# HGRN2 decays inside the chunk: differences of cumulated sums on VectorE, or sums by TensorE with constant 0/1 matrices

## The chip, the cores and the metric

One core of one Trainium2 chip runs the whole program. The metric is device microseconds from start to end of an execution; the median of three runs is quoted. Weights and constants lie in DRAM when the clock starts.

## The reference, cut to what matters

Two layers of a diffusion backbone over 512 latent and 256 context tokens, width 1024. In each layer a combined projection feeds four mixers of four heads of 64 channels: HGRN2, RWKV-7, windowed attention and latent attention. HGRN2 is a gated linear attention in both directions, computed in chunks of 64 tokens:

```python
bc = jnp.cumsum(blocks(logf), axis=-2)            # log decays, cumulated within a chunk
def step(S, inp):
    qb, kb, vb, bb = inp
    inter = jnp.einsum('bhtk,bhkv->bhtv', qb * jnp.exp(bb), S)
    rel = jnp.where(causal, bb[:, :, :, None, :] - bb[:, :, None, :, :], -jnp.inf)
    att = jnp.einsum('bhtk,bhsk,bhtsk->bhts', qb, kb, jnp.exp(rel))
    o = inter + jnp.einsum('bhts,bhsv->bhtv', att, vb)
    b_end = bb[:, :, -1:, :]
    S = jnp.exp(b_end[:, :, 0, :, None]) * S + jnp.einsum('bhsk,bhsv->bhkv', kb * jnp.exp(b_end - bb), vb)
    return S, o
```

The second layer needs no output for context tokens, only their states.

## The kernel before, in words

The channels lie on the partitions and the tokens along the free axis. `mixers` (line 1279) runs a layer's mixer half. It projects (TensorE, weights split in two parts for three-pass products), and `hg_gates` (889) makes log decays and keys of both directions; line 926 cumulates the decays within chunks with a scan. Then, in pools opened at line 1437, `weave` (243) traces several streams side by side: RWKV forward and RWKV backward (`rw_dir`, one step each per round), HGRN (`hgrn`, 0.44 step per round in the first layer and 0.36 in the second), the preparation of the attentions, and in the first layer the rest of the modulation vectors (`ada`). The place of an instruction in an engine's queue comes from a scheduler that takes the traced order as priority; a queue is worked in order. The next stage (the attentions and the read-out, from line 1462 on) opens its PSUM pool when the streams have ended; its first products are those of line 338.

RWKV (`rw_pair` 685, `rw_chain` 795) inverts triangular matrices of two chunks by doubling: per level products of a<-TP,Gm, a copy into the padded AP (607), products a<-AP,TT, the update of TU (781), its turn on TensorE (312) and copies (785, 791).

HGRN (`hgrn` 928) goes through six segments of four chunks, three per direction, the context segment first. Per segment:

- keys scaled to the end of their chunk: a difference (962), an exponential (963), a product (964), turned on TensorE to `ket` (968 to 971); `ef`, the exponential of the cumulated decays (966);
- if output is wanted, six levels (976): for level h the causal pairs whose tokens lie in the later and the earlier half of a block of 2h tokens. A difference against a reference token of each block (983), two exponentials of the two halves (995, 996), the keys' product (997), the queries' product into the padded operand XQ, one instruction per partition half (1000), the products of scores in PSUM (1013), and a masked copy into `att` (1015). Level 0 takes pairs with the diagonal (987 to 990, 1003 to 1008);
- the states of the four chunks (1020 to 1029) and the output (1032 to 1044).

"Padded" means that an operand holds both head halves along a further free index and is zero where that index is not the partition half, so that the whole array contracts. HGRN's PSUM tag `hg` has two buffers of one bank; the attentions' preparation and `ada` draw on it as well. The program's float32 products show up as two records each in the trace, a turn as one.

Of the kernel before, what the change touches and what calls it, by code (L numbers as in the profile page):

```python
# [11 lines left out]
F32 = mybir.dt.float32  # L12
# [22 lines left out]
# columns of the per-layer parameter block  # L35
# [4 lines left out]
# columns of the constant block  # L40
# [4 lines left out]
NCST = C_BAND + 256  # L45


def _consts():
    """Constants that depend on shapes alone."""
# [40 lines left out]
    for n, cc, sc in ((64, C_COS, C_SIN), (32, C_COSM, C_SINM)):  # L90
# [3 lines left out]
        for p in range(128):  # L94
            d = p % n
            ang = pos[d // (n // 2)] * inv[d % nf]
            c[p, cc:cc + 512] = np.cos(ang)
            c[p, sc:sc + 512] = np.sin(ang)
    c[:, C_BAND:C_BAND + 128] = np.where(i[None, :] >= i[:, None], 0.0, -1e30)
# [4 lines left out]
def _col_tiles():  # L104
    """Column tiles (lists of w_in columns) that are computed channels x tokens, and the token-major group."""
# [17 lines left out]
# heads 0, 2, 1, 3  # L123
# [6 lines left out]
def _pack(inp):  # L130
# [7 lines left out]
    # shifts and scales of two channel tiles side by side  # L138
# [84 lines left out]
class Ker:  # L223
# [19 lines left out]
    def weave(*gens):  # L243
        """Traces several streams side by side: (generator, steps at a time)."""
# [31 lines left out]
    def gemm_col(s, ps, parts, act, segs):  # L276
        """ps[:, tokens] = weights^T act for one tile of 128 output channels.  parts: (first k, tiles) of the weights."""
# [7 lines left out]
    def gemm_last(s, m, *a):  # L285
        """Column m; the last one a segment after the other, as the norm of the first begins beside the second."""
# [3 lines left out]
    def gemm_cols(s, cols, act, ks=range(KT)):  # L290
        """The same for several column tiles (psum, parts, segments) together, k by k."""
# [8 lines left out]
    def diag(s, out, lhsT, rhs, start=True, stop=True):  # L300
        """64 x 64 products of the two partition halves, each with its own half."""
# [3 lines left out]
    def dtrans(s, out, x, idm):  # L305
        """64 x 64 transposes of the two partition halves."""
# [24 lines left out]
    def seg_gemm(s, lhsT, rhs, ntok, use, tag=None):  # L331
        """use(columns, psum) for each segment of lhsT^T rhs; lists of operands are summed."""
# [46 lines left out]
    def setup_masks(s):  # L379
        """The constants that the recurrences need."""  # L380
# [7 lines left out]
        # masks of the pairs that hold the diagonal as well  # L388
# [31 lines left out]
    def ada_rest(s, tp, room):  # L420
        """The first layer's second half and the second layer, a channel tile at a time, without the tensor engine.
        s.adaw(): where the weights of a tile go."""
# [4 lines left out]
        for n in range(72):  # L427
# [4 lines left out]
            # the second layer's context goes no further than its keys  # L432
# [12 lines left out]
    def sumsq(s, m, n, pool, x=None, eng=None):  # L445
        """Adds the squares of channel tile m of the residual to s.acc."""
# [31 lines left out]
    def norm(s, l, mod, sh, sc, gcol, wp, rs, hhi, hlo, ks, ts=None):  # L478
        """Channel tiles ks of the normalised and modulated residual in two parts; ts: room for two tiles."""
# [18 lines left out]
    def proj(s, l, cols, eng=None):  # L498
        """Column tiles (number, tokens) of the input projection into PSUM (channels x tokens); several at once go k by k."""
# [4 lines left out]
    def proj_tok(s, l, it, vt):  # L504
        """HGRN inputs and window values, tokens on partitions."""
# [39 lines left out]
    def rw_prep(s, l, last, g, tp):  # L545
        """Everything of the RWKV mixer that needs no state."""
# [34 lines left out]
        # values, centred over the channels of their head, tokens on partitions  # L581
# [9 lines left out]
        # bonus: (sum over the head of r k r_k) v  # L591
# [1379 lines left out]
```

## Time and profile before

| | us |
|---|---|
| runs, median (lowest to highest) | 2637.68 (2636.43 to 2646.11) |
| span of the profiled execution | 2644.5 |
| TensorE matmul busy | 2408.1 (91%) |
| VectorE busy | 1660.6 (63%) |
| ScalarE busy | 1227.3 (46%) |
| GpSimd busy | 484.9 (18%) |

The profiled execution is a run of its own; what lies around its span is not recorded beside it. Busy times are unions over the whole span and mix stages with different limits. L12 is line 12 of the kernel; PE and PEld are TensorE's matmuls and weight loads, DVE VectorE, ACT ScalarE, POOL GpSimd, SP the queue that issues most transfers. A group's row gives the count, the busy time, the mean length of one in ns, and after the second bar the engine's idle time just before, with what ended it.

### The profile page before, as it was taken

How to read it: one execution, taken by the hardware profiler on the slowest of the kernel's cores; microseconds unless marked ns; L12 is line 12 of the kernel's file. 1: busy time of each engine (PE TensorE's matmuls, PEld its weight loads, DVE VectorE, ACT ScalarE, POOL GpSimd, SP SyncE). 2: the span in 40 equal slices, each digit the busy share in tenths (PEclk: the TensorE clock that was granted, in tenths of full speed). 3: DMA queues.
4: the chain of work that ended last, by engine and by line, in shares of the span. 5: the costliest groups of instructions: out<-in, count | busy, mean ns of one | idle time of the engine just before them, and what ended most of it. 6: DMA issues, size and time to landing. Idle time of an engine off the chain costs nothing. (4 is left out here: it accounts for less than half of the span.)

```text
span 2644.5 us, 46379 instructions
## 1 busy us (share of the span) xinstructions
PE 2408.1 (91%) x18131; PEld 1998.6 (76%) x18131; DVE 1660.6 (63%) x3055; ACT 1227.3 (46%) x2331; POOL 484.9 (18%) x613
## 2 busy tenths in 40 slices
PE   6999788879998999999999997888996999999994
PEld 3889666656586888888888786666674898899993
DVE  5573598777578644344336746876745667667765
ACT  4373356546723211211234654664653556555653
POOL 1010464441011000000020005654102000000002
PEclk9999899989998999999999998998998899999997
DMA  6223110111053433334322130001113888888885
GB/s 245 65 89 111 49 34 20 30 65 57 1 178 129 144 112 120 117 116 132 118 81 64 57 116 13 20 16 49 56 36 107 267 270 270 280 265 264 260 277 179
DMA packets 161026, 322.46 MB, mean 122 GB/s; under 512 B 12288, under 2 KB 84736, under 8 KB 160800
## 3 DMA queue, kind: packets, MB, share of 16 engines
q1 hardware_dynamic: 153744, 293.60, 34.2%
q0 software_dynamic: 6480, 23.73, 2.5%
q8 instruction: 144, 2.36, 0.4%
q10 hardware_dynamic: 576, 2.10, 0.2%
q14 instruction: 82, 0.67, 0.1%
HBM read 295.39 MB, written 22.54 MB: 120 GB/s over the span
## 5 line engine op out<-in xcount | busy, mean ns | idle before, releaser
L272 PE MATMUL big<-hhi,hiw 128*128 128x512 f32 (+1 forms) x1504 | 520.8, 347 | 9.1 <-ACT hhi L491 4.6
L273 PE MATMUL big<-hlo,hiw 128*128 128x512 f32 (+1 forms) x1504 | 523.6, 348 | 2.4 <-DVE hlo L492 2.4
L274 PE MATMUL big<-hhi,low 128*128 128x512 f32 (+1 forms) x1504 | 519.5, 346 | 5.8 <-DVE low L260 3.9
L259 ACT CAST hiw<-raww 128x512 fp32r<-128x512 f32 (+3 forms) x208 | 158.4, 769 | 616.9 <-PE big L273 413.4
L272 PEld LDWEIGHTS big<-hhi,hiw 128*128 128x128 f32 x1504 | 286.2, 191 | 53.2 <-ACT hhi L491 5.7
L274 PEld LDWEIGHTS big<-hhi,low 128*128 128x128 f32 x1504 | 286.2, 190 | 45.1 <-DVE low L260 5.6
L273 PEld LDWEIGHTS big<-hlo,hiw 128*128 128x128 f32 x1504 | 286.4, 190 | 41.0 <-DVE hlo L492 4.2
L260 DVE TENSOR_TENSOR lom<-rawm,him 128x1024 fp32r<-128x1024 f32 x176 | 215.1, 1225 | 128.0 <-ACT him L259 126.7
L260 DVE TENSOR_TENSOR low<-raww,hiw 128x512 fp32r<-128x512 f32 (+3 forms) x196 | 177.3, 909 | 161.1 <-ACT hiw L259 160.8
L259 ACT CAST him<-rawm 128x1024 fp32r<-128x1024 f32 x176 | 184.3, 1047 | 150.4 <-PE sml L273 60.7
L272 PE MATMUL sml<-xh,him 128*128 128x256 f32 x528 | 152.0, 288 | 0.0
L273 PE MATMUL sml<-xl,him 128*128 128x256 f32 x528 | 149.5, 283 | 0.0
L274 PE MATMUL sml<-xh,lom 128*128 128x256 f32 x528 | 149.4, 283 | 0.0
L260 DVE TENSOR_TENSOR lov<-rawv,hiv 128x1024 fp32r<-128x1024 f32 x88 | 107.5, 1222 | 38.2 <-ACT hiv L259 37.8
L272 PE MATMUL sml<-him,xh 128*128 128x256 f32 x440 | 127.4, 290 | 0.7 <-DVE xl L260 0.6
L273 PE MATMUL sml<-lom,xh 128*128 128x256 f32 x440 | 125.4, 285 | 0.0
L274 PE MATMUL sml<-him,xl 128*128 128x256 f32 x440 | 125.3, 285 | 0.0
L273 PE MATMUL big<-gl,hiw 128*128 128x512 f32 (+1 forms) x352 | 119.5, 339 | 0.0
L272 PE MATMUL big<-gh,hiw 128*128 128x512 f32 (+1 forms) x352 | 118.9, 338 | 0.0
L274 PE MATMUL big<-gh,low 128*128 128x512 f32 (+1 forms) x352 | 118.2, 336 | 0.0
L259 ACT CAST hiv<-rawv 128x1024 fp32r<-128x1024 f32 x88 | 92.4, 1050 | 51.3 <-PE y L274 41.5
L757 POOL TENSOR_TENSOR Gm<-G,mskf 128x256 f32<-128x256 f32 x120 | 99.5, 836 | 85.7 <-PE a L612 82.5
(560 smaller groups left out, 5633.7 us busy)
## 6 DMA issues: line engine op xcount, KB each, us to landing
rawm<-in_m SPq DMA_DIRECT2D x176, 512.0 KB, 5.1
rawv<-in_m SPq DMA_DIRECT2D x88, 512.0 KB, 4.7
raww<-in_wadt SPq DMA_DIRECT2D x56, 512.0 KB, 3.5
raww<-in_w SPq DMA_DIRECT2D x52, 512.0 KB, 3.9
raww<-in_winc SPq DMA_DIRECT2D x92, 256.0 KB, 2.8
raww<-in_wout SPq DMA_DIRECT2D x16, 512.0 KB, 4.1
wadt<-in_wadt SPq DMA_DIRECT2D x16, 512.0 KB, 4.4
raww<-in_w SPq DMA_DIRECT2D x16, 448.0 KB, 3.3
```

Source lines behind the costliest of these rows:

```text
L259: s.S.copy(hi, src)
L260: (eng or s.V).tensor_sub(lo, src, hi)
L272: s.E.matmul(out, ah, bh, start=start, stop=False)
L273: s.E.matmul(out, ah, bl, start=False, stop=False)
L274: s.E.matmul(out, al, bh, start=False, stop=stop)
L757: P.tensor_mul(x, G[:, :, 0, :, 0], s.mskf[:, 1 - d, i][:, None, None].to_broadcast(sh))
```

## The change

The constants gain, for each direction, eight 0/1 matrices of 128 x 128 (C_LV). The log decays are no longer cumulated. Per segment they are turned to tokens on partitions (`lt`), and a product of `lt` with one of the matrices gives, for two chunks and all channels, the sum of the decays that a token needs: of a level, from the block's reference to the token (always the way that makes it a decay), of the whole chunk up to it (6), or from it to the chunk's end (7). Exponentials read these sums from PSUM. Those of the queries are written into both partition halves of the padded operand, whose halves change places in the layout, and one product over 128 partitions multiplies the queries in, in place. The keys' exponentials go to one of two zeroed tiles XK. The queries hq are laid out by segment. The matrices of one direction are in SBUF at a time; the second direction's replace them after the third segment's levels. Three buffer counts fall: `dd` 3 to 2, the transposed keys of RWKV in the second layer 4 to 3, the weights of `ada` 3 to 1. Comments are struck throughout.

```diff
-                V.tensor_tensor_scan(r(zd[:, t]), r(s.rst[:, d]), r(zd[:, t]), 0.0, OP.mult, OP.add)
...
+        lvl = levels(0)
+        XK = itertools.cycle(s.zeroed(tp, [128, 2, 256], "XK", 2))
...
+                pl = psh().rearrange("p (a n) -> p a n", n=128)
+                for a in range(4):
+                    s.turn(pl[:, a], lf[d][:, a // 2, o + 128 * (a % 2):o + 128 * (a % 2) + 128])
+                lt = tp.tile([128, 4, 128], F32, name="lt")
+                S.copy(lt, pl)
+                def decays(i):
+                    ps = psh()
+                    for a in range(4):
+                        E.matmul(ps[:, 128 * a:128 * a + 128], lt[:, a], lvl[:, i], start=True, stop=True)
+                    return ps.rearrange("p (t n) -> p t n", t=2)
...
-                V.tensor_tensor(dc, bc[:, :, :, end:end + 1].to_broadcast([128, 2, 4, 64]), bc, OP.subtract)
-                S.activation(dd, dd, AF.Exp)
+                S.activation(dc, ch4(decays(7)), AF.Exp)
...
-                S.activation(ef, bs, AF.Exp)
+                S.activation(ef, decays(6), AF.Exp)
...
-                        V.tensor_tensor(x.rearrange("p t (b n) -> p t b n", n=2 * h), br,
-                                        br[:, :, :, e:e + 1].to_broadcast([128, 2, 128 // h, 2 * h]), OP.subtract)
+                        pd = decays(li)
+                        x = next(XK)
...
-                            S.activation(xw[:, :, :, d], xw[:, :, :, d], AF.Exp, scale=-1.0)
-                            S.activation(xw[:, :, :, 1 - d], xw[:, :, :, 1 - d], AF.Exp)
-                            V.tensor_mul(xw[:, :, :, d], xw[:, :, :, d], w(ks)[:, :, :, d])
+                            S.activation(w(x, d), w(pd, d), AF.Exp)
                             for p in range(2):
                                 hp = slice(64 * p, 64 * p + 64)
-                                V.tensor_mul(XQ[hp, :, p].rearrange("p t c (b h) -> p t (c b) h", h=h),
-                                             xw[hp, :, :, 1 - d], w(qs)[hp, :, :, 1 - d])
+                                S.activation(XQ[hp, p].rearrange("p t c (b h) -> p t (c b) h", h=h), w(pd, 1 - d)[hp], AF.Exp)
+                            V.tensor_mul(w(x, d), w(x, d), w(ks, d))
+                            xq = XQ.rearrange("p q t c (b h) -> p q (t c b) h", h=h)
+                            qw = qs.rearrange("p t (b e h) -> p (t b) e h", e=2, h=h)[:, :, 1 - d]
+                            V.tensor_mul(xq, xq, qw[:, None].to_broadcast([128, 2, 256 // h, h]))
+                        ps = psh()
...
+                if d == 0 and sg == 1:
+                    lvl = levels(1)
```

`levels(d)` is one transfer of 512 KB from the constants on SP's queue.

## Rows read from the trace of the kernel before

**Rows 1.** Stretches: length, busy us of PE, PEld, DVE, ACT, POOL; PEclk; DMA.

```profile
286.00:590.00 304.00, 246.74 (x3404) 185.62 (x3402) 253.04 (x602) 160.82 (x456) 160.90 (x223) 0.92 0.12 39
240.00:270.00 30.00, 30.00 (x172) 26.15 (x171) 4.20 (x7) 6.76 (x13) 2.17 (x4) 1.00 0.21 79
1598.00:1850.00 252.00, 207.72 (x2910) 158.93 (x2909) 198.90 (x510) 143.43 (x415) 143.94 (x209) 0.93 0.07 22
```

**Rows 2.** Waits, 286 to 590 us: who for whom, total us, times, longest.

```profile
ACT TP L785 <- DVE TU L781: 24.7, 21, 2.3
ACT AP L607 <- DVE AP L607: 21.5, 17, 3.3
...
PEld hg L612 <- DVE XQ L1000: 11.3, 16, 1.6
```

**Rows 3.** Timeline of PE: start, length, records merged.

```profile
499.45 0.44 PE L312 MATMUL a<-cst,TU 128*128 128x128 f32 x2
...
603.88 0.65 PE L312 MATMUL pt<-cst,xm 128*128 128x128 f32 x4
```

**Rows 4.** By line, ends of both stretches: ns min/median/max, first and last start.

```profile
L1074 DVE TENSOR_TENSOR hz<-hq,XQ x2: 684/686/689, 576.2 to 576.9; 64x512 f32<-64x512 f32 x2
...
L338 PE MATMUL sc<-xm,ARf x24: 379/538/1222, 580.2 to 599.0; 128*128 128x512 f32 x12, 128*128 128x256 f32 x12
...
L1074 DVE TENSOR_TENSOR hz<-hq,XQ x2: 673/682/690, 1831.7 to 1833.1; 64x512 f32<-64x512 f32 x2
...
L338 PE MATMUL sc<-xm,ARf x12: 592/592/1222, 1846.9 to 1859.8; 128*128 128x512 f32 x12
```

**Rows 5.** Groups of VectorE, first layer's recurrences, 286 to 590 us.

```profile
L1000 DVE TENSOR_TENSOR XQ<-dd,hq 64x256 f32<-64x256 f32 x60 | 36.9, 616 | 1.2 <-ACT dd L996 0.6
L983 DVE TENSOR_TENSOR dd<-hz 128x512 f32<-128x512 f32 x36 | 30.0, 834 | 3.0 <-PE hg L312 2.6
...
L962 DVE TENSOR_TENSOR dd<-hz 128x512 f32<-128x512 f32 x6 | 4.3, 723 | 0.0
```

**Rows 6.** Groups of VectorE, second layer's recurrences, 1598 to 1850 us.

```profile
L983 DVE TENSOR_TENSOR dd<-hz 128x512 f32<-128x512 f32 x24 | 20.4, 850 | 0.3
L1000 DVE TENSOR_TENSOR XQ<-dd,hq 64x256 f32<-64x256 f32 x40 | 19.1, 477 | 0.5
...
L962 DVE TENSOR_TENSOR dd<-hz 128x512 f32<-128x512 f32 x6 | 4.3, 712 | 0.1
```

**Rows 7.** Groups, whole span: the scans ahead of the recurrences.

```profile
L926 DVE TENSOR_TENSOR_SCAN hz<-rst,hz 128x768 f32<-128x768 uint8 x8 | 14.0, 1755 | 0.2
```

**Rows 8.** Groups of TensorE, 286 to 590 us.

```profile
L612 PE MATMUL hg<-XQ,dd 128*64 128x64 f32 x480 | 23.9, 241 | 9.9 <-DVE XQ L1000 9.7
...
L312 PEld LDWEIGHTS a<-cst,TU 128*128 128x128 f32 x120 | 13.1, 146 | 16.4 <-DVE TU L781 10.2 <-issue 2.5 <-DVE att L1015 0.5
```

**Rows 9.** Groups of ScalarE, 286 to 590 us.

```profile
L995 ACT ACTIVATE dd<-dd 128x256 f32<-128x256 f32 x30 | 12.6, 422 | 9.9 <-DVE dd L983 9.7
...
L971 ACT COPY ket<-hg 128x512 f32<-128x512 f32 x6 | 3.5, 586 | 5.8 <-PE hg L312 5.7
```

**Rows 10.** Transfers and SP's waits, 286 to 590 us (issue, size, us to landing).

```profile
wada<-in_wada SPq DMA_DIRECT2D x8, 512.0 KB, 4.8
...
SPq L1420 <- PE hg L1178: 45.2, 1, 45.2
```

**Rows 11.** Timeline of VectorE, first layer: start, length.

```profile
462.24 0.44 DVE L1015 COPY_PREDICATED att<-msk,hg 128x256 f32<-128x256 uint8 x1
...
479.68 0.75 DVE L962 TENSOR_TENSOR dd<-hz 128x512 f32<-128x512 f32 x1
...
494.32 0.69 DVE L983 TENSOR_TENSOR dd<-hz 128x512 f32<-128x512 f32 x1
494.93 0.73 DVE L1015 COPY_PREDICATED att<-msk,hg 128x256 f32<-128x256 uint8 x1
...
498.99 0.43 DVE L1015 COPY_PREDICATED att<-msk,hg 128x256 f32<-128x256 uint8 x1
```

More of the change, by code (lines that the diff above doesn't have):

```diff
@@ L44 @@
 C_BAND = C_SINM + 512
-NCST = C_BAND + 256
+C_LV = C_BAND + 256
+NCST = C_LV + 2048
 def _consts():
@@ L98, in _consts @@
             c[p, sc:sc + 512] = np.sin(ang)
+    u, v = i[:, None], i[None, :]
+    same = (u // 64) == (v // 64)
+    lv = [(u == v) & (v % 2 == 1)]
+    for h in LVL[1:]:
+        m = (v // (2 * h)) * 2 * h + h
+        lv.append(((v >= m) & (u >= m) & (u <= v)) | ((v < m) & (u > v) & (u < m)))
+    lv += [same & (u <= v), same & (u > v)]
+    lv = np.stack(lv, axis=1)
+    c[:, C_LV:C_LV + 2048] = np.stack([lv, lv[::-1, :, ::-1]], axis=1).reshape(128, 2048)
     c[:, C_BAND:C_BAND + 128] = np.where(i[None, :] >= i[:, None], 0.0, -1e30)
@@ L746, in rw_pair @@
         yield
-        bkt = tp.tile([128, 2, 2, 2, 64], F32, name="bkt", bufs=4 if last else 3)
+        bkt = tp.tile([128, 2, 2, 2, 64], F32, name="bkt", bufs=3)
         pb = psa().rearrange("p (c q h n) -> p c q h n", c=2, q=2, h=2)
@@ L918, in hg_gates @@
             zd = z[d]
-            r = (lambda x: x[:, ::-1]) if d else (lambda x: x)
             for t in range(2):
@@ L925, in hg_gates, with hgrn, levels @@
                 V.tensor_add(zd[:, t], zd[:, t], tmp)
-                V.tensor_tensor_scan(r(zd[:, t]), r(s.rst[:, d]), r(zd[:, t]), 0.0, OP.mult, OP.add)
-    def hgrn(s, last, q, b, key, it, O, tp):
+    def hgrn(s, last, q, lf, key, it, O, tp):
         E, V, S, P = s.E, s.V, s.S, s.P
+        def levels(d):
+            x = tp.tile([128, 8, 128], F32, name="lvl")
+            s.Q.dma_start(x, s.I['cst'][:, C_LV + 1024 * d:C_LV + 1024 * d + 1024].rearrange("p (a b) -> p a b", a=8))
+            return x
+        lvl = levels(0)
         XQ, = s.zeroed(tp, [128, 2, 2, 4, 32], "XQ")
         QE, = s.zeroed(tp, [128, 4, 2, 2, 64], "QE")
+        XK = itertools.cycle(s.zeroed(tp, [128, 2, 256], "XK", 2))
         s.scr = [x.rearrange("p a b c n -> p (a b c n)") for x in (XQ, QE)]
@@ L976, in hgrn @@
                     for li, h in enumerate(LVL):
-                        ps = psh()
-                        x = tp.tile([128, 2, 256], F32, name="dd", bufs=3)
-                        e = (d if li == 0 else h if d else h - 1)
-                        br = bs.rearrange("p t (b n) -> p t b n", n=2 * h)
-                        V.tensor_tensor(x.rearrange("p t (b n) -> p t b n", n=2 * h), br,
-                                        br[:, :, :, e:e + 1].to_broadcast([128, 2, 128 // h, 2 * h]), OP.subtract)
+                        pd = decays(li)
+                        x = next(XK)
                         if li == 0:
-                            y = tp.tile([128, 2, 256], F32, name="dd", bufs=3)
-                            S.activation(y, x, AF.Exp)
-                            S.activation(x, x, AF.Exp, scale=-1.0)
+                            y = tp.tile([128, 2, 256], F32, name="dd", bufs=2)
+                            S.activation(y, pd, AF.Exp)
+                            S.activation(x, pd, AF.Exp, scale=-1.0)
                             V.tensor_mul(x, x, ks)
@@ L1040, in hgrn @@
                         V.tensor_add(od, pv, od)
-                        s.head_squares(O, 0, 4 * sg, 4 * sg + 4, tp.tile([128, 2, 256], F32, name="dd", bufs=3)
+                        s.head_squares(O, 0, 4 * sg, 4 * sg + 4, tp.tile([128, 2, 256], F32, name="dd", bufs=2)
                                        .rearrange("p a (b n) -> p (a b) n", n=64).rearrange("p (c t) n -> p c t n", t=2))
@@ L1400, in modulation @@
                     if l == 0:
-                        yield s.ada(range(4, 6), lambda: tp.tile([128, 2, 512], F32, name="wada", bufs=3),
+                        yield s.ada(range(4, 6), lambda: tp.tile([128, 2, 512], F32, name="wada"),
                                     lambda: s.ps("hg", 512, 2), lambda: tp.tile([128, 512], F32, name="adams")), 6 / 122
@@ L1445, in mixers @@
                     s.weave(*((s.rw_dir(d, last, g, rwt, *done, bp, tp, ARs, None if d else first), 1) for d in range(2)),
-                            (s.hgrn(last, hq, hz, hk, it, hgt, tp), 0.36 if last else 0.44), (attention_prep(psf), 0.5), *modulation(tp))
+                            (s.hgrn(last, hqs, hz, hk, it, hgt, tp), 0.36 if last else 0.44), (attention_prep(psf), 0.5), *modulation(tp))
             with ExitStack() as ox:
```

17 lines of the change are left out of this document (8 added, 9 removed).

## Prediction

> **What bounds the kernel now.** The stretches come first, since the edit lives in two of them: the recurrences of the first layer (286 to 590 us) and of the second (1598 to 1850). In both VectorE is busy for 253.0 of 304 and 198.9 of 252 us, 83% and 79%, and TensorE shows 246.7 and 207.7 us [rows 1]. Two full-looking engines, so the next question is which of them others wait for. The waits of the first layer answer: ScalarE stands 24.7 us behind VectorE's update of RWKV's inverse (TU) and 21.5 us behind its half of the padded copy (AP), and TensorE's weight loads 11.3 us behind the padded queries of HGRN (XQ) [rows 2]. VectorE is the nearest thing to a bound, with TensorE close behind. TensorE's busy time holds the run-out of small products: two turns of 128 columns in a row show 0.44 us, four show 0.65 [rows 3], so one more record costs 0.105 us and the run-out is about 0.23. Weight loads alone take 185.6 of 304 us [rows 1].
>
> The Trainium skill, "Perfetto Trace Analysis", section "Identifying the Most-Contended Engine", says that the busy share of matmuls misjudges how much room the engine has and that the weight loads' share is to be read. By the matmul share the added records would leave the first stretch almost no room (289.5 of 304 us, the second rival's time, 2646); by the other one they leave a fifth of it (185.6 + 408 x 0.146 = 245), which goes with the forecast.
>
> Three streams run side by side there: RWKV forward, RWKV backward, HGRN. Which ends last? In the first layer the rotated queries that follow HGRN are done at 577.6 us (the last row's start plus its length) and the next stage's first product starts at 580.2; in the second 1833.8 against 1846.9 [rows 4]. So HGRN with what hangs on it has 2.6 and 13.1 us to spare: close to being the last itself.
>
> **The change, part by part.**
>
> VectorE loses the differences of cumulated decays: 36 and 24 of them by level, 30.0 and 20.4 us [rows 5, 6], and 6 and 6 for the keys, 4.3 and 4.3 us. The padded queries are written by 60 and 40 products over 64 partitions now, 36.9 and 19.1 us; 30 and 20 in-place products over 128 partitions and 512 elements take their place, which I price like the differences of the same size, 0.834 and 0.850 us: 25.0 and 17.0. Together VectorE loses 30.0 + 4.3 + 11.9 = 46.2 us in the first layer and 20.4 + 4.3 + 2.1 = 26.8 in the second, 73 in all. Its share in the first stretch falls to 207 of 304, 68%.
>
> The eight cumulating scans ahead of the recurrences, 1.755 us each [rows 7], go too. I take nothing for them: the input projection fills TensorE for 30.00 of 30 us while VectorE does 4.20 [rows 1]; were that cover gone, 14.0 us.
>
> TensorE gains, in each of 12 segments, four turns of one record (120 records stand for 120 turns) and groups of four products, two records each (480 for 240 products) [rows 3, 8]: eight groups in ten segments, two in the two context segments of the second layer that need no output. That is 6 x (4 + 64) = 408 records and 4 x 68 + 2 x 20 = 312; at 0.105 us 42.8 and 32.8 us, 75.6 in all. A group of eight is 0.84 us plus the run-out, 1.07 us, and there are 60 + 24 = 84 groups.
>
> ScalarE gains one exponential in each of the 50 upper levels (two halves of the partitions instead of one instruction), 0.42 us each, and 12 copies of turned decays like today's 0.586 us [rows 9]: 12.7 + 3.5 = 16.2 us in the first layer, on top of 160.8 of 304. That lies beside other work; I add nothing for the engine. That exponentials read from PSUM might be dearer or cheaper no row shows; the copy of 512 elements from PSUM at 0.586 us is the nearest, and it leaves the price alone (ends: a few us of ScalarE either way, hidden).
>
> The constants: two loads of 512 KB a layer on SP's queue; such a load takes 4.8 us to land [rows 10]. The first is issued when the stage opens, so HGRN starts some 5 us later than now. The second waits until the third segment's levels have read the first; between the last level of that segment (462.2) and the first difference of the next direction (479.7) lie 17 us [rows 11], which hide it, unless it stands on SP behind another load that waits: one waits 45.2 us for TensorE [rows 10]. Ends: 0 and, since that wait is for products which are done before 479.7, a few us; I take 0. The modulation weights fall from three buffers to one: eight loads [rows 10] that then alternate with their products, some 8 x 4.8 = 38 us of loading within 304, and nothing in the recurrences needs the result; 0, with an upper end of one landing, 4.8 us, where TensorE stands in front of one. Zeroing the two new operands on GpSimd at the start lies beside the first load. The second layer's fourth buffer of transposed keys goes; the first layer runs the same code with three, so 0; upper end 11.5 us, if each of five later pairs of chunks waits as long as the longest wait for an update of TU, 2.3 us [rows 2].
>
> The sum. Saved VectorE time becomes saved time in full only if VectorE stays the bound: -73. TensorE's added time becomes lost time in full only if TensorE is the bound and stays idle as long as now: +75.6. Between these ends I take half of the first, because at 68% VectorE is no longer a standing queue and what remains between RWKV's steps is their own latency: -36.5. From the second: a group of 1.07 us in front of somebody costs half its length, 84 x 0.53 = 44.9 us over the streams, and every second hit falls on the stream that ends last: +22. Net -14.5. The profiled execution's span is 2644.5 us, which stands 6.8 us above the median of the runs (2637.7) and inside their spread; from the median I get **2623 us**. The granted clock was 0.92 and 0.93 in the two stretches [rows 1], that is, TensorE spent part of them at the lower level; with more products it should fall there no more often than now. I count nothing.
>
> **Rivals.**
>
> *VectorE was all of it.* If both streams shrink with VectorE's work, 73 us go: 2565. For it: waits behind VectorE lead rows 2. Against it: the doubling steps of RWKV are chains through three engines.
>
> *TensorE takes VectorE's place.* If every group, not every second one, delays the stream that ends last: -36.5 + 44.9 = +8, 2646. For it: 246.7 + 42.8 = 289.5 of 304 us busy. Against it: the weight loads' share.
>
> *HGRN ends last* (the other side). Today a level's chain starts on VectorE, which can run ahead while TensorE does RWKV's products. After it, a level goes TensorE, ScalarE, VectorE, TensorE, VectorE, each group of decays takes one of HGRN's two PSUM buffers ahead of the scores, and ScalarE may not write the padded queries before the level before has read them. In series a level gains 1.07 + 0.42 and loses a difference, 0.69 where nothing stretches it [rows 11]: +0.8 us, where two levels are 4.1 us apart now (494.93 to 498.99). A segment's head gains turns 0.65, copy 0.59, a group 1.07 and loses 0.72: +1.6. First layer: 30 x 0.8 + 6 x 1.6 = 34 us against 2.6 to spare; second 20 x 0.8 + 6 x 1.6 = 26 against 13.1: together +44, 2682; with half of it overlapped 14 + 0, 2652. It decides from 0.1 us a level in the first layer, if no other delay of HGRN's is relieved; but HGRN's own VectorE work per level falls by the difference and from 1.23 to 0.83 us for the queries [rows 5], and its products wait on VectorE now too [rows 2].
>
> That the change doesn't do what it says is hardly possible: the instructions are struck from the program.
>
> **How the numbers follow.** A change under 0.5%, 13.2 us, can't be told from none here: faster means under 2624.5, slower over 2650.9. Forecast 0.42 (own range 2608 to 2638): 0.28 faster, 0.14 same. VectorE all of it 0.14, all faster. TensorE takes its place 0.18: 0.01 faster, 0.13 same, 0.04 slower. HGRN last 0.26: 0.05 same, 0.21 slower. Together 0.43, 0.32, 0.25. The range 2592 to 2668 leaves out the lower part of the second case and the upper part of the last, about 0.1 each. Cases of both signs hold much of the chance, hence the forecast's own range above.
>
> **What would show it.** In the profile after: VectorE's busy time in the two stretches down by about 46 and 27 us; 84 groups of eight records with full weights reading the new tile, 0.1 us apart; ScalarE up by about 16 us in the first layer; both stretches shorter by some 9 and 5 us. If the padded products take much more than 0.85 us, the first term was wrong. If VectorE idles far more while TensorE's products wait for ScalarE's exponentials and HGRN's last sum comes after RWKV's, the last rival holds. If TensorE's weight loads fill the stretch, the second does. If both stretches shrink by 20 us and more, VectorE was the bound alone.

## The result, and the profile after

The changed kernel takes 2699.16 us, median of 4 runs (2696.28 to 2702.11), against 2640.51 of the kernel before beside it: 58.6 us more, ratio 1.0228 with a 95% interval of 1.0207 to 1.0248. It is slower; the forecast was 2623 us, and the measured time lies above the range. The profiled execution took 2697.78 us with a span of 2696.0.

The two stretches of recurrences in the profile after, each up to the next stage's first product (engines and columns as in [rows 1]; the same two lines for the kernel before follow, cut at the same events to within a us, since [rows 1] goes a few us beyond):

```profile
286.00:611.00 325.00, 286.06 (x3785) 223.45 (x3784) 204.60 (x510) 173.93 (x490) 153.13 (x217) 0.97 0.11 33
1630.00:1896.00 266.00, 233.75 (x3208) 186.91 (x3208) 173.91 (x456) 153.71 (x440) 137.07 (x205) 0.99 0.08 23
```

```profile
286.00:580.00 294.00, 238.39 (x3376) 180.76 (x3374) 244.86 (x582) 157.81 (x450) 153.85 (x214) 0.92 0.10 33
1598.00:1847.00 249.00, 204.72 (x2904) 157.48 (x2902) 196.93 (x506) 142.65 (x413) 140.94 (x204) 0.93 0.07 20
```

The first stretch grew from 294 to 325 us, the second from 249 to 266: 48 of the span's 51.5 us (2696.0 less 2644.5). VectorE lost 40.3 and 23.0 us (46 and 27 were said) and is now busy for 63% of the first stretch. TensorE's records rose by 409 and 304 (408 and 312 were counted), its busy time by 47.7 and 29.0, to 88% of both stretches. The scans that fell away ahead of the recurrences left no mark, as was said: before 286 us, and between the two stretches, the traces keep their length within 1 us.

The terms of the sum, one by one, in the groups of the first layer's stretch (out<-in, shapes, count | busy us, mean ns | idle before). They answer to [rows 5], [rows 8] and [rows 9]:

```profile
L1025 DVE TENSOR_TENSOR XQ<-XQ,hq 128x512 f32<-128x512 f32 x30 | 24.8, 828 | 0.7 <-ACT XQ L1021 0.2
L1022 DVE TENSOR_TENSOR XK<-XK,xm 128x256 f32<-128x256 f32 x30 | 15.9, 532 | 15.1 <-ACT XK L1018 14.9
L1013 DVE TENSOR_TENSOR XK<-XK,xm 128x512 f32<-128x512 f32 x6 | 7.8, 1293 | 0.2
...
L986 PE MATMUL hg<-lvl,lt 128*128 128x128 f32 x384 | 56.3, 290 | 0.2
...
L1021 ACT ACTIVATE XQ<-hg 64x256 f32<-64x256 f32 x60 | 22.3, 372 | 0.7
L1018 ACT ACTIVATE XK<-hg 128x256 f32<-128x256 f32 x30 | 11.7, 389 | 16.5 <-PE hg L986 15.9
```

The padded products took 24.8 us (25.0 was said), ScalarE is busy 16.1 us more (16.2 was said). These prices of the parts were right; what they were worth was not.

TensorE's timeline in the first layer (start, length, records merged) shows the groups between the other streams' small products, 1.16 us each with the run-out (1.07 was said from [rows 3]):

```profile
358.74 0.38 PE L820 MATMUL c<-Z,AR 128*64 128x64 f32 x4
359.04 1.16 PE L986 MATMUL hg<-lvl,lt 128*128 128x128 f32 x8
360.13 0.33 PE L820 MATMUL c<-Z,AR 128*64 128x64 f32 x2
...
365.46 1.16 PE L986 MATMUL hg<-lvl,lt 128*128 128x128 f32 x8
366.55 0.44 PE L624 MATMUL c<-rwvt,bkt 128*64 128x128 f32 x4
```

The waits of that stretch (who for whom: total us, times, longest) answer to [rows 2], where ScalarE stood behind VectorE:

```profile
POOL Gm L769 <- PE a L624: 49.8, 22, 7.2
...
ACT AP L619 <- DVE AP L619: 18.8, 20, 2.9
DVE AP L619 <- PE a L624: 17.7, 13, 4.0
ACT TP L797 <- DVE TU L793: 17.4, 21, 2.7
ACT XK L1018 <- PE hg L986: 15.9, 19, 1.8
...
DVE XK L1022 <- ACT XK L1018: 14.9, 14, 2.2
DVE TU L793 <- PE a L624: 12.7, 13, 2.9
```

In the kernel before, over the 294 us cut above, GpSimd's wait for TensorE was already the longest in total, and VectorE's waits for TensorE in RWKV's lines were small:

```profile
POOL Gm L757 <- PE a L612: 40.8, 19, 5.7
...
DVE TU L781 <- PE a L612: 3.9, 10, 0.8
DVE G L727 <- PE a L612: 3.9, 10, 1.0
DVE AP L607 <- PE a L612: 3.8, 8, 1.2
```

ScalarE's waits for VectorE (AP, TP) became only a little smaller. Beside them VectorE now waits for TensorE in RWKV's lines (AP, TU), and ScalarE waits 15.9 us for the decay sums, on which VectorE's key product of the level then waits 14.9. Who ends last did not change. In the first layer (duration ns min/median/max, first and last start):

```profile
L1101 DVE TENSOR_TENSOR hz<-hq,XQ x2: 683/686/689, 606.6 to 607.3; 64x512 f32<-64x512 f32 x2
```

```profile
L846 DVE TENSOR_TENSOR xm<-c,xm x12: 270/290/292, 383.3 to 610.3; 128x128 f32<-128x128 f32 x12
```

The last rotated queries are done at 608.0 (the last row's start plus its length), 2.7 us before the next stage's first product at 610.7 (2.6 before the change, [rows 4]); RWKV's last sum ends at 610.6. In the second layer the last rotated queries end at 1885.2 and the next product starts at 1896.2, 11.0 us later (13.1 before). All three streams were stretched together.

### The profile page after: what moved, and what is told of

It reads as the page before. It is cut to its first block, busy times and chain, and to the rows that moved or that the text cites. A ratio compares the mean times of both kernels' runs of the same rounds, so it can differ in the third digit from the quotient of the medians.

```text
span 2696.0 us, 47776 instructions
## 1 busy us (share of the span) xinstructions
PE 2486.0 (92%) x18851; PEld 2070.3 (77%) x18851; DVE 1585.4 (59%) x2925; ACT 1254.3 (47%) x2398; POOL 480.4 (18%) x617
```

## The experiments

Two theories stood against each other. **Theory 1:** TensorE is so full that the added records delay all three streams. **Theory 2:** the longer chain of a level (TensorE, ScalarE, VectorE, TensorE, and two PSUM buffers) is what costs, whatever TensorE has to do. Smaller buffers and the products in place were side issues. Each time below stands beside runs of the kernel before on the same chip, and "less" or "more" is the difference of the two medians.

### The side issues

In place alone. The exponentials of the queries go straight into the padded operand:

```diff
-    S.activation(xw[:, :, :, 1 - d], xw[:, :, :, 1 - d], AF.Exp)
...
-        V.tensor_mul(XQ[hp, :, p]..., xw[hp, :, :, 1 - d], w(qs)[hp, :, :, 1 - d])
+        S.activation(XQ[hp, p]..., xw[hp, :, :, 1 - d], AF.Exp)
...
+    V.tensor_mul(xq, xq, qw[:, None].to_broadcast([128, 2, 256 // h, h]))
```

> The kernel before with one part of the change alone: the queries' exponentials are written into the two halves of the padded operand by ScalarE, and one VectorE product in place fills it; decay sums stay with VectorE and no product is added to TensorE. Saves VectorE 12 x 30 = some 11.9 us per 30 levels in the first layer and a little in the second (25.0 against 36.9 us, 17.0 against 19.1), ScalarE pays about what the second half costs it. Theory 1 (the added products hold up all three streams on TensorE): this part is innocent, the time is that of the kernel before or up to 10 us less (2628 to 2642). Theory 2 (the longer chain of a level, TensorE to ScalarE to VectorE, decides): the same, as no part of that chain is in it. Rival (writing and multiplying in place is itself slow because the halves are now two passes behind one another): 10 us or more slower than before.

Measured 2640.18 us, 2.5 less, ratio 0.9991 (0.9982 to 1.0001). VectorE's 12 us of the first layer bought nothing that can be told from none.

The smaller buffers alone:

```diff
-    name="bkt", bufs=4 if last else 3
+    name="bkt", bufs=3
...
-    name="wada", bufs=3
+    name="wada"
```

> The kernel before with the change's smaller buffer counts alone (the second layer's key operands 3 in place of 4, the modulation weights 1 in place of 3). All theories on TensorE: 2640 to 2646. Rival (the smaller buffers cost part of the 58 us): 5 us or more above before, in the first layer for the weights, in the second for the operands.

Measured 2639.34 us, ratio 0.9999 (0.9989 to 1.0009): the zero that the prediction gave these edits holds.

### TensorE's records without anybody who waits for them

First in the kernel before, with VectorE's work left as it is:

```diff
+def extra(ps):
+    for a in range(4):
+        E.matmul(ps[:, 128 * a:128 * a + 128], s.bo, s.cen, start=True, stop=True)
...
 ps = psh()
+extra(ps)
```

> The kernel before plus only TensorE's work of the change: each level's group of four products of 128x128x128 in full float32 into the level's own PSUM buffer, two such groups and four transposes ahead of the turns of the keys; nobody reads them, and VectorE keeps all the work that the change takes from it. Theory 1 (TensorE's added records delay every stream): slower than before by at least the 58 us that the change lost, 50 to 100 us, that is 2690 to 2740 (VectorE's relief is missing here). Theory 2 (the chain of the level decides, TensorE's records as such are cheap): within 15 us of before, 2640 to 2655.

Measured 2670.62 us, 28.0 more, ratio 1.0116 (1.0090 to 1.0142). Neither number: more than theory 2 allows, half of what theory 1 asked. Then in the changed kernel, where VectorE has been relieved, with the exponentials taking another operand:

```diff
-    pd = decays(li)
+    decays(li)
+    pd = lf[d][:, :, o:o + 256]
```

> The changed kernel, but the exponentials read the log decays in SBUF instead of the decay sums in PSUM: all products of the decays are still made, nobody waits for them; ScalarE and VectorE do what they do in the changed kernel (the values are not the decays). Theory 1: no gain to speak of, 2680 to 2705. Theory 2: most of the 58 us comes back, 2630 to 2655, or less than before.

Measured 2672.38 us, 29.7 more than before, ratio 1.0117 (1.0094 to 1.0141). So the wait is worth half of the 58.6 us, and the other half stays without it. "The wait" stands here for all that goes with reading the sums, also that their PSUM bank is held until ScalarE has read it. That this is 2672 and the run ahead of it 2671 is the most telling pair: with the groups in place VectorE's whole relief, with what ScalarE does more for it, is worth nothing. The pair is not quite pure, as the first one's groups read constants and write the bank of the level's own scores. Now without the groups:

```diff
-    for a in range(4):
-        s.turn(pl[:, a], lf[d][...])
-    lt = tp.tile([128, 4, 128], F32, name="lt")
-    S.copy(lt, pl)
...
-    pd = decays(li)
+    pd = lf[d][:, :, o:o + 256]
```

> The changed kernel without any of TensorE's decay products and transposes (the exponentials read the log decays in SBUF, as in e3_free, so the values are not the decays): only VectorE's relief is left. What the runs so far say: TensorE's products alone cost 28 us (e2_peload), taking away the wait for them gives back 27 (e3_free against the changed kernel). Theory A (the prediction's term, VectorE's 73 us are worth half): 2600 to 2610. Theory B (VectorE's relief is worth nothing, since with it e3_free is no faster than e2_peload without it): 2635 to 2650. Theory C (VectorE was the bound, but TensorE takes its place when the products are there): 2570 to 2600.

Measured 2614.12 us, 25.1 less than before, ratio 0.9897 (0.9879 to 0.9916). Between the expected 2600 to 2610 and 2635 to 2650: VectorE's 73 us are worth a third of their length, and only while TensorE gets nothing for them. ScalarE's added exponentials are in this number. The stretches of these three (columns as above), the one with groups under an unrelieved VectorE:

```profile
286.00:586.00 300.00, 272.70 (x3784) 218.30 (x3782) 239.39 (x581) 159.07 (x450) 154.40 (x214) 0.99 0.11 33
```

with groups under a relieved one:

```profile
286.00:590.00 304.00, 278.12 (x3772) 221.02 (x3770) 199.64 (x510) 177.55 (x489) 151.76 (x217) 0.98 0.12 36
```

and relieved without groups:

```profile
286.00:557.00 271.00, 230.12 (x3363) 172.67 (x3362) 200.02 (x510) 174.08 (x483) 152.52 (x217) 0.95 0.13 40
```

In the first two TensorE is busy for 91% of the stretch, and it makes no difference whether VectorE has 239 or 200 us to do. In the third the stretch is 33 us shorter than in the second.

Is it the records, or that a group is there at all (its PSUM tile, its place in TensorE's order)? A quarter of the records, and all of them without a PSUM tile of their own:

```diff
-    for a in range(4):
+    for a in range(1):
         E.matmul(ps[:, 128 * a:128 * a + 128], lt[:, a], lvl[:, i], start=True, stop=True)
```

> e3_free with the first of each group's four products alone: 2 records in place of 8, the same groups, PSUM tiles and transposes, and nobody waits (the values are not the decays). So far without the wait: no groups 2614, half the records 2663, all of them 2672. If TensorE's record time sets the cost, with a quarter of the records: 2628 to 2640. If a group costs by being there (its PSUM tile, its place in TensorE's order): 2650 to 2665.

```diff
-def decays(i):
-    ps = psh()
+def decays(i, ps):
...
+    ps = psh()
+    decays(li, ps)
...
-    ps = psh()
```

> e3_free with all of its records, but each group writes the PSUM tile that the level's own scores use after it, and the two groups at a segment's start that of the turned keys: no PSUM tile more than in the kernel before. If the added PSUM tiles (two buffers for twice as many) cost: 2625 to 2650. If TensorE's time does: 2665 to 2675, as e3_free.

Measured 2633.73 us (7.8 less than before, 0.9947 to 0.9975) and 2666.66 us (25.1 more, 1.0065 to 1.0109). It is the records' time: a quarter of them costs 17.3 us over the kernel without groups (25.1 less 7.8), all of them 54.8 (25.1 and 29.7), and still 50.2 (25.1 and 25.1) without PSUM tiles of their own, so those cost a few us at most.

### The same with the wait in place

The same chain with single-pass products of rounded operands, half the records. The log decays lose low bits:

```diff
-    x = tp.tile([128, 8, 128], F32, name="lvl")
+    x = tp.tile([128, 8, 128], F32R, name="lvl")
...
-    lt = tp.tile([128, 4, 128], F32, name="lt")
+    lt = tp.tile([128, 4, 128], F32R, name="lt")
```

> The changed kernel with the transposed log decays and the 0/1 matrices as rounded float32 operands that TensorE takes in a single pass: the same chain from TensorE to ScalarE to VectorE and the same buffers, with one record in place of four records per product (720 added records fall to some 200; log decays lose their low bits). Theory 1: two thirds or more of the loss comes back, 2610 to 2655. Theory 2: little comes back, 2680 to 2700.

Measured 2696.41 us, 53.8 more than before, ratio 1.0200 (1.0170 to 1.0229). The expectation counted four records a product where the trace shows two in the changed kernel, so 384 records are left and not some 200. A record costs 0.112 us: eight of them show 1.16 us in the timeline above, two show 0.49 in one further down. On its face theory 1 is dead: 336 records of 0.112 us, 37.6 us of TensorE, are gone, and 4.8 us came back. The granted clock speaks against that reading (the first number after the engines' busy times):

```profile
286.00:606.00 320.00, 274.88 (x3593) 208.77 (x3591) 204.17 (x510) 175.42 (x493) 152.51 (x217) 0.93 0.11 34
1624.00:1897.00 273.00, 235.51 (x3065) 185.79 (x3065) 174.01 (x456) 155.19 (x445) 136.87 (x206) 0.91 0.08 22
```

It is 0.93 and 0.91 here, 0.97 and 0.99 in the changed kernel, so TensorE stood at its lower level for more of the time. Full-speed time lost is 0.07 x 320 + 0.09 x 273 = 47.0 us here and 0.03 x 325 + 0.01 x 266 = 12.4 there, 34.6 more: about what the records saved. A profile is one execution of several. The record has the mean granted clock of every run over its whole span; one less the clock, times the span, is on average 100.3 us here and 72.8 there, 27.5 more. So most of what the records saved went with the clock by either count. The same half of the records without the wait (the values are not the decay sums):

```diff
-    pd = decays(li)
+    decays(li)
+    pd = lf[d][:, :, o:o + 256]
```

> e4_f32r with the exponentials reading SBUF: half of the added TensorE records (single pass) and no wait for them. Beside e3_free (2672, all records, no wait) and e7_relief (no records). If TensorE's records set the time, halfway between those two; if the granted clock gives back what fewer records save, as in e4_f32r (0.93 and 0.91 in the two stretches against 0.97 and 0.99 of the changed kernel), at e3_free's 2672 with a clock below 0.95.

Measured 2662.80 us, 23.6 more than before, ratio 1.0087 (1.0069 to 1.0105), with 0.95 and 0.93. Halfway it is not: 48.7 us over the kernel without groups, of 54.8 for all of them. The wait is worth 30.2 us at half of the records (53.8 less 23.6) and 28.9 at all of them (58.6 less 29.7).

To tell the record count from the single-pass form, each product is made twice, one upon the other. (A split of the log decays into two rounded parts, meant for the same question, leaves 80.7 KB a partition of SBUF where a later pool needs 82, so it has no time.)

```diff
-    for a in range(4):
-        E.matmul(ps[:, 128 * a:128 * a + 128], lt[:, a], lvl[:, i], start=True, stop=True)
+    for a in range(8):
+        E.matmul(ps[:, 128 * (a % 4):128 * (a % 4) + 128], lt[:, a % 4], lvl[:, i], start=True, stop=True)
```

> e4_f32r with each of its products made twice, one upon the other: as many TensorE records per group as the changed kernel, in the single-pass form, nothing else added. If the records count and e4_f32r's gain was taken back by the granted clock: 2694 to 2706, with the clock at 0.96 or more in both stretches. If the form is what is slow: 2715 or more. If neither records nor clock count with the wait in place: 2690 to 2700 with the clock of e4_f32r.

Measured 2730.70 us, 90.6 more than before, ratio 1.0351 (1.0332 to 1.0370). The 336 records put back cost 36.8 us (90.6 less 53.8), their 37.6 us of TensorE nearly in full: with the wait in place records count one for one here. And with the record count of the changed kernel this one is 32 us slower, at a clock of 0.93 and 0.94:

```profile
286.00:619.00 333.00, 294.71 (x3784) 232.48 (x3783) 199.71 (x510) 175.44 (x493) 149.42 (x216) 0.93 0.11 33
1637.00:1927.00 290.00, 243.12 (x3214) 194.85 (x3214) 175.48 (x456) 155.74 (x445) 138.28 (x206) 0.94 0.07 21
```

0.07 x 333 + 0.06 x 290 = 40.7 us of full speed lost against 12.4, 28.3 of the 32 (33.0 by the clocks of all runs). So the form was slow, as the second expectation had it, and the clock's rows account for most of it.

Last, the wait almost by itself: one single-pass record of 512 columns per group, which fills the bank that ScalarE reads (the values are not the decay sums):

```diff
-    for a in range(4):
-        E.matmul(ps[:, 128 * a:128 * a + 128], lt[:, a], lvl[:, i], start=True, stop=True)
+    E.matmul(ps, lt[:, 0], lvl.rearrange("p a b -> p (a b)")[:, :512], start=True, stop=True)
```

> The changed kernel with one single-pass record of 512 columns per group in place of four products (it fills the whole bank, so that ScalarE waits for it and reads it as before; the values are not the decay sums). The wait is in place and TensorE almost relieved of the change. Without the wait a quarter of the records cost 20 us over e7_relief's 2614. If the wait costs its 20 to 33 us whatever TensorE has to do: 2645 to 2665. If it costs because TensorE is full, and the decay sums come late: 2618 to 2638, under the kernel before.

Measured 2677.01 us, 37.0 more than before, ratio 1.0134 (1.0117 to 1.0151). That is above both expectations: 62.1 us over the kernel without groups. On TensorE such a record stands for as long as the quarter's two records, 0.43 us to the next record's start against 0.42. Here (start, length)

```profile
371.39 0.50 PE L989 MATMUL hg<-lvl,lt 128*128 128x512 f32 x1
371.82 0.32 PE L624 MATMUL c<-rwvt,G 128*64 128x128 f32 x1
```

and in the kernel with a quarter of the records

```profile
344.95 0.49 PE L986 MATMUL hg<-lvl,lt 128*128 128x128 f32 x2
345.37 0.34 PE L624 MATMUL a<-AP,TT 128*64 128x64 f32 x4
```

and ScalarE's wait is as long as in the changed kernel, though the group is one record:

```profile
ACT XK L1021 <- PE hg L989: 17.3, 17, 3.6
```

Again the clock is in the number, 0.93 and 0.92. The table takes it out for the whole series. "Clock" and "lost" (TensorE's full-speed time lost to the lower level, summed over both stretches as above) are those of the profiled executions. The last column goes by all runs, because one execution can lie off its kernel's others: the profiled one of the 512 columns took 2688.01 us, 11 above the median. It is an estimate: the mean of each run's time less its loss, (1 - clock) x span, set against the same for the kernel without groups, 2533.3 us. The kernel before comes out between 2546.8 and 2547.6 beside every experiment. Runs of one kernel mostly spread by 2 to 4 us by this reckoning, so a difference of some 4 us between two rows tells nothing. What moved the clock, the wait or the records, the column does not say.

| records per group, form | wait | us against before | over "no groups" | clock | lost, us | over "no groups", clock taken out |
|---|---|---|---|---|---|---|
| none | no | -25.1 | 0 | 0.95, 0.96 | 23.1 | 0 |
| 2, two-record form | no | -7.8 | 17.3 | 0.97, 0.97 | 15.8 | 25.8 |
| 4, single pass | no | +23.6 | 48.7 | 0.95, 0.93 | 33.1 | 39.2 |
| 8, two-record form | no | +29.7 | 54.8 | 0.98, 0.96 | 16.7 | 64.0 |
| 1 of 512 columns, single pass | yes | +37.0 | 62.1 | 0.93, 0.92 | 43.7 | 49.7 |
| 4, single pass | yes | +53.8 | 78.9 | 0.93, 0.91 | 47.0 | 61.6 |
| 8, two-record form (the change) | yes | +58.6 | 83.7 | 0.97, 0.99 | 12.4 | 93.0 |
| 8, single pass | yes | +90.6 | 115.7 | 0.93, 0.94 | 40.7 | 92.1 |

With the clock taken out the steps are in order. Without the wait the cost grows with TensorE's added time, and falls behind it at the full count: 216 records (two for each of 84 groups and 48 turns) of 0.112 us are 24.2 us, against 25.8; 384 are 43.0 against 39.2; 720 are 80.6 against 64.0. The two kernels with eight records and a wait agree, 93.0 and 92.1. And the wait costs 23.9 us at the lightest group (49.7 less 25.8), 22.4 at half, 29.0 at the full one. So both theories have their part: the wait costs 22 to 29 us, nearly the same at a group as short as a quarter as at the full one, and the records cost on top of it.

The same reckoning bears on VectorE's relief. The kernel before stands 13.9 us over "no groups" with the clock taken out (2547.2 less 2533.3), so 11 of the relief's 25.1 us went with a higher granted clock. The groups under an unrelieved VectorE come out at 2599.0 us and those under a relieved one at 2597.3, again the same.

### Can the wait be taken away?

Each level's products issued one level ahead, into a bank of their own; RWKV's two streams share a bank to make room:

```diff
+def psk():
+    return s.ps("dk", 512, 1)
...
-    pd = decays(li)
+    pd = nd
...
+    if li + 1 < len(LVL):
+        nd = decays(li + 1, psk)
     yield
...
-    return s.ps("c" + nm)[:, :128].rearrange("p (t n) -> p t n", t=2)
+    return s.cc[:, 256 * d:256 * d + 128].rearrange("p (t n) -> p t n", t=2)
```

> The changed kernel, whole, with each level's decay products issued one level ahead into a PSUM bank of their own (the two streams of the other recurrence share one bank for their small products to make room): TensorE has made them long before ScalarE asks. Theory 2 (the wait from TensorE to ScalarE costs what e3_free gave back): 2665 to 2680, some 25 us under the changed kernel. Rival (e3_free was faster because ScalarE reads SBUF faster than PSUM, or because its products had no reader): 2690 to 2705.

Measured 2692.55 us, 53.4 more than before, ratio 1.0195 (1.0176 to 1.0214). The wait is still there, a level ahead or not:

```profile
ACT XK L1023 <- PE dk L989: 21.4, 19, 2.2
```

Two controls tell what the shared bank itself does, one in the changed kernel and one in the kernel before, both with the freed bank as a third buffer for HGRN:

```diff
-    s.ps("hg", 512, 2)
+    s.ps("hg", 512, 3)
```

> The changed kernel with three buffers for HGRN's PSUM tiles in place of two (the other recurrence's two streams share a bank). If the two buffers hold the level's chain up (theory 2, the modulation vectors keep one of them for long in the first layer): 2665 to 2685, the gain in the first layer. If TensorE's time and the wait as such cost: 2690 to 2700, like e8_pipe, which had a bank for the decay sums alone.

> The kernel before with the same three PSUM buffers and the shared bank: what the sharing itself costs or a third buffer gives without the change. If sharing a bank between the two streams costs, e8_pipe and e12_hg3after are to be read with that deducted: over 2646. If it is free: 2630 to 2642.

Measured 2713.51 us (72.0 more, 1.0247 to 1.0293) and 2651.40 us (9.9 more, 1.0019 to 1.0059). Sharing and a third buffer together cost some 10 us in the kernel before, and the two lie 62.1 apart, much like the change's own 58.6. So a third buffer bought in this way gives nothing; what it would give without the shared bank was not tried. Beside the control with the same sharing, issuing ahead gains 18.6 us (72.0 less 53.4), of which the shared bank takes the larger part back: 5.2 us are left against the change (58.6 less 53.4). Since ScalarE's wait is as long as before in the trace, this run does not show how much of the wait's 29 us can be had.

### A version that beats both?

VectorE's relief is worth 25 us if TensorE pays nothing. GpSimd is busy for half of the stretch; it could pay:

```diff
-    V.tensor_tensor(x.rearrange("p t (b n) -> p t b n", n=2 * h), br,
+    (P if li in (1, 3, 5) else V).tensor_tensor(x.rearrange("p t (b n) -> p t b n", n=2 * h), br,
```

> e1_inplace (the kernel before with the queries' exponentials and products in place) with the differences of three of the six levels made by GpSimd: VectorE gives up 12 us in place and 15 us of differences in the first layer, about 2 and 10 in the second, some 39 us in all, and TensorE gets nothing. GpSimd's products of the same shape take 1317 ns against VectorE's 834. If VectorE's relief is worth what e7_relief shows (25 us for 73, a third): 13 us under before, 2624 to 2632. If GpSimd's longer operations on the level's chain cost that: 2638 to 2650.

> The same with all six levels' differences on GpSimd: some 64 us less for VectorE, near e7_relief's 73. At a third of it 21 us under before, 2616 to 2628, if GpSimd (some 150 of 294 us busy before, 40 more then) still has room; if it becomes the bound or delays the other recurrence's own GpSimd work in its queue: 2640 or more.

Measured 2648.26 us (6.2 more, 1.0020 to 1.0043) and 2653.45 us (11.4 more, 1.0041 to 1.0072). In the second, the differences on GpSimd:

```profile
L983 POOL TENSOR_TENSOR dd<-hz 128x512 f32<-128x512 f32 x36 | 40.8, 1137 | 11.2 <-PE hg L612 3.9 <-ACT UP L607 3.9 <-DVE QE L948 2.8
```

VectorE fell to 221 us in that stretch and the kernel got slower. That GpSimd's 1137 ns in place of VectorE's 834 stand on the level's chain may be the reason; it was not tested apart from GpSimd's fuller queue (154 us busy before, 192 here). No version tried with the right values beats the kernel before by more than its measurement can tell; the products in place alone equal it.

## Why the prediction was wrong

The sum took half of VectorE's relief and a quarter of TensorE's added time as two terms that add, and the wait for the decay sums at nothing. That is where it failed. The balance in measured steps from the kernel before: VectorE's relief, -25.1; the groups that nobody reads, +54.8; the wait for them, +28.9; together +58.6. The steps are differences of neighbouring runs, so they close by themselves, and their order matters: with the groups first, they cost 28.0, the relief then +1.7, the wait 28.9. In either order relief and groups together cost 29.7 us where the sum had -14.5, a miss of 44.2. The wait is another 28.9. Of the 76 us between forecast and result the rest, some 3, is the kernel before, 2640.5 beside the change and 2637.7 in the prediction. Against the prediction's own steps:

**The bound.** VectorE was read as the nearest thing to a bound, TensorE as close behind. The first half holds so far as it goes: relieving VectorE alone shortens the kernel. The second half decided. TensorE was not close behind but the next bound at once: 28.0 us for the groups under an unrelieved VectorE, 29.7 under a relieved one, so that VectorE's relief is worth nothing beside them. The rows had a sign of it. "Waits behind VectorE lead rows 2" is not so: the row that leads the same list is GpSimd's wait for RWKV's products on TensorE, 40.8 us (shown above), and [rows 2] begin below it. Whether that wait lies on a path that ends last, no run shows.

**VectorE's term.** The instructions went as counted: the lines of the change fell from 93.2 us (36.9 + 30.0 + 17.9 + 4.3 + 4.1) to 48.5 (24.8 + 15.9 + 7.8) in the first layer. Half of 73 us, 36.5, was taken as gained. Alone it gained 25.1, a third, of which some 11 went with the granted clock; beside the groups it gained nothing.

**TensorE's term.** The price of a record was nearly right (0.112 us for 0.105, a group 1.16 for 1.07), and so was the count. Then the sum halved it twice, half of a group's length for a hit and every second hit on the stream that ends last: +22. Measured +28.0 while VectorE is unrelieved, and +54.8 without a wait where it is relieved, 0.65 us for each of 84 groups. With the wait in place the records of one experiment were paid at 98% of their length (36.8 of 37.6 us). The premise that only the stream that ends last pays did not hold: in the first layer HGRN and RWKV, which the change does not touch, both ended 30.4 us later (577.6 to 608.0, 580.2 to 610.6). TensorE was busy for 81% of the first stretch before (238.39 of 294 us), and all three streams run through its order.

The rule that the forecast leaned on, in the Trainium skill's "Perfetto Trace Analysis", section "Identifying the Most-Contended Engine", is that TensorE's room is to be read by the share of its weight loads (and by the share of its peak arithmetic), not by its matmuls' row. By the loads the first stretch after the change still has 31% of room (223.45 of 325 us are taken). The trace does not bear the rule out here: with the matmuls' row at 88% and the loads' at 70% of the stretch (294.71 and 232.48 of 333 us, the kernel with each product made twice), records added with the wait in place were paid nearly in full, 36.8 of 37.6 us.

**ScalarE and the chain.** ScalarE's instructions were priced rightly and hidden as said. What was missing from the sum is the wait: ScalarE asks for a decay sum that stands behind other streams' products in TensorE's order. That was only in the rival "HGRN ends last". It measured 28.9 us, 22 to 29 with the clock taken out.

**Loads, buffers, GpSimd's zeroing.** The zero of the transposed keys' and the modulation weights' buffers was tested and holds. The constants' loads were not tried apart; the trace shows 0.4 us of TensorE behind them in the second layer.

**The rivals.** "VectorE was all of it" is refuted by the kernel without groups: 2614, not 2565. "TensorE takes VectorE's place" was the right mechanism, but priced at 2646 with one group's half length each; the kernels with groups and no wait stand at 2671 and 2672. "HGRN ends last" named the right extra chain and a range that began at 2652, but its place was wrong: HGRN has as much slack at the end as before in the first layer (2.7 us against 2.6), in the second 11.0 against 13.1, and RWKV, which the change does not touch, grew as much. It was a rival with TensorE's rival switched off; both came together, and the time lies above either.

**The clock.** "No more often than now" was right for the change: 0.97 and 0.99 against 0.92 and 0.93. By the two profiled executions that is some 29 us of full-speed time given back by the clock (0.08 x 294 + 0.07 x 249 = 41.0 us lost before, 12.4 after), by the clocks of all runs some 20 (91 to 96 us lost in the kernel before, 72.8 after). It was counted as nothing; without it the change would have lost more.

What stays open: along which queue the wait reaches RWKV. In the kernel whose groups nobody reads, ScalarE idles as long before the exponentials (12.3 and 9.3 us behind TensorE's last reading of XQ and XK), and that one is faster. So ScalarE's standing alone is not the path, and no run separates it from the later products of the level on TensorE.

## What to carry to other kernels

Work moved from one well-filled engine to another does not pay as two terms that add: here the relief was worth a third of what VectorE lost while TensorE had nothing added, and nothing once it had. Before such a move, load the receiving engine alone with the new instructions, unread, and relieve the giving engine alone: two runs that give both terms, and the two together in a third that shows whether they add. And price the new wait by where its producer stands in a shared in-order engine, not by the producer's own length: one record behind the other streams' products kept ScalarE waiting as long as eight did.

## What the runs showed of the hardware that was not expected

The single-pass form of the same products went with a lower granted clock: 0.93 and 0.94 at the full record count, against 0.97 and 0.99 with the two-record form, 0.112 us from record to record in both; 32 us of time between them. Which property of the form does it was not tried.

A product of 128 x 512 elements on VectorE took 1293 ns in the mean on the new operand XK (L1013 above, 692 to 1651) where the same product took 673 to 693 before (L989); that is 3.7 us more in the first layer. It is not the operand: two of the six took 692 and 693 ns, and each of the other four, 1437 to 1651 ns, began while GpSimd was at a product of padded queries (L965) and ended 0.55 us after that one ended, as here (start, length):

```profile
304.40 1.71 POOL L965 TENSOR_TENSOR QE<-dd,hq 64x512 f32<-64x512 f32 x1
```

```profile
305.22 1.44 DVE L1013 TENSOR_TENSOR XK<-XK,xm 128x512 f32<-128x512 f32 x1
```

None of the six of the kernel before stood beside such a one in the first layer. No run tried the two apart.

The exponentials of 128 x 256 elements took 389 ns from PSUM (L1018 above) and 423 from SBUF in the kernel whose groups nobody reads, so reading PSUM was not the dearer side:

```profile
L1021 ACT ACTIVATE XK<-hz 128x256 f32<-128x256 f32 x30 | 12.7, 423 | 9.9 <-PE hg L624 9.3
```
